# Modulation blocks as row dot products on DVE, another cost table for the planner, and an earlier normalization of the first tile in the last stage

## The chip, the cores and the metric

The kernel runs on one core of a Trainium2 chip. The metric is the device time of one execution in microseconds. The kernel before was timed in three runs.

## The reference

The input is a sequence of 256 tokens with 1024 features, `x`, a conditioning vector `c`, memory tokens and the weights, all float32. Two blocks of two layers each follow one another. In the first block each layer `i` is conditioned by `c`; this is the part that the change touches:

```
sc = jax.nn.silu(c)
for i in range(2):
    mod = sc @ w_ada[i] + b_ada[i]                  # 6 blocks of 1024
    sh_m, sc_m, g_m, sh_f, sc_f, g_f = split(mod, 6)
    h = rms_norm(x, norm_mix[i]) * (1 + sc_m) + sh_m
    y = moba_attention(h, ...) if i == 0 else short_conv(h, w_in, conv_w, w_out)
    x = x + g_m * y
    h = rms_norm(x, norm_ffn[i]) * (1 + sc_f) + sh_f
    x = x + g_f * swiglu(h, w_gate_up[i], w_down[i])
```

The second block has two layers with a gated linear recurrence and a stick-breaking attention, each with a memory attention beside it, a projection, a layer norm, and a mixture of 16 experts with a layer norm. The last layer norm gives the output.

## The kernel before

The 256 tokens are two tiles, T0 and T1, of 128 rows (`x0` and `x1` in the trace and the order). Both go through eight stages: attention, first FFN, short conv, second FFN, recurrence, first MoE, stick-breaking attention, second MoE. All weights come from DRAM as 556 units of 128x1024 floats (512 KB each) on SP's queue into a ring of buffers; `pump` issues the loads. A dense unit (`raw`) is split in two fp32r parts: ACT casts it to `hi`, DVE subtracts to get `lo` (line L487 is the helper `tt`). A product is then three fp32r matmuls, of `hi` with both parts of the left side and of `lo` with its first part. Left sides are made from a tile by `modnorm`: ACT squares the tile with an accumulated sum, DVE, POOL (a power) and DVE again scale it, PE transposes it in two times four 128x128 pieces, ACT applies scale and shift from `mcol`, and ACT's cast and a DVE subtraction split it.

Which instruction an engine gets next is decided before the run, by a planner in Python, `Sched`. Each part of the work is a generator that yields conditions; the planner keeps a clock `now` for PE and further clocks `tA`, `tD` for ACT and DVE, and `dma_t` for the loads, adds a cost for each instruction it emits (`mm` and `tr` for PE, `pump` for a load), and always continues the part that can go on first by these clocks. The costs are a table of numbers written into those functions. The order so found is fixed; on the chip each engine runs its own list in order, and semaphores make it wait for the others.

`ada_task` makes the modulation `mod`, in twelve blocks (i, j) of 1024 outputs. Five blocks, `ADA_PE`, go through PE as they are. For the other seven, (0,5) and all six of layer 1, each of the eight units of a block holds 128 of the 1024 input rows; DVE multiplies a unit by the matching column of `cs` = silu(c) and adds it to a sum `dst` of 128x1024. The sum over the 128 partitions is left to PE: for shifts and scales with eight 128x1 matmuls against a column `one`, four for each half block (the trace shows 64 for four blocks in eight sets), after which DVE adds the bias and writes `mcol`; for the gates ((0,5), (1,2), (1,5)) POOL first clears `dst` and loads the bias into a row of it, and each half is split (ACT, DVE) and multiplied twice with `ones`, so that the sum stands in all partitions.

The last stage ends with two layer norms: for T0 in `affine_pool` (normalization on ACT, then gain and bias of the left half on POOL and of the right half on DVE), for T1 in `affine_rows` (four operations on DVE); `moe` starts them.

Of the kernel before, what the change touches and what calls it, by code (L numbers as in the profile page):

```python
# [9 lines left out]
F32R = mybir.dt.float32r  # L10
# [14 lines left out]
GATES = (2, 5)  # L25
# [136 lines left out]
def host_arrays(inp):  # L162
# [3 lines left out]
    for i in range(2):  # L166
        for j in range(6):
            w = np.ascontiguousarray(g["w_ada"][i][:, j * D:(j + 1) * D])
            u[f"ada{i}_{j}"] = _split_units(w) if (i, j) in ADA_PE else w.reshape(8, 128, 1024)
# [27 lines left out]
    rows = np.stack([rowsrc[s] for k, (s, i) in zip(plan.kind, plan.src) if k == "row"])  # L197
# [104 lines left out]
class Body:  # L302
# [28 lines left out]
    def start(self, again):  # L331
# [21 lines left out]
        self.rawdense = 0  # L353
        self.hl_used = 0
# [96 lines left out]
    def mm(self, out, lhsT, rhs, start, stop, shared=False):  # L451
        self.nc.tensor.matmul(out, lhsT, rhs, start=start, stop=stop, skip_group_check=shared)  # L452
        n = 1
        for d in rhs.shape[1:]:
            n *= d
        m = out.shape[0]
        if lhsT.dtype == F32R:
            c = max(0.227 * n / 512, 0.108)
        else:
            c = max(0.86 * n / 512, 0.224 if m > 64 else 0.112) * (0.26 if m <= 32 and n == 512 else 0.52 if m <= 64 and n == 512 else 1.0)  # L460
        self.sch.now += c

    def tr(self, out, in_):
        self.nc.tensor.transpose(out, in_, self.ident)  # L464
        self.sch.now += 0.109
# [71 lines left out]
    def pump(self):  # L537
        while self.can_dma():
# [18 lines left out]
            self.dma_t = max(self.dma_t, self.sch.now) + 1.3  # L557
# [141 lines left out]
    def ada_task(self):  # L699
        for i in range(2):  # L700
            order = [(j, (b,)) for b in range(2) for j in (1, 0)] if i == 0 else [(1, (0, 1)), (0, (0, 1))]
            for j, halves in order + [(j, (0, 1)) for j in (2, 4, 3, 5)]:
                uid = self.ids[f"ada{i}_{j}"]
                gate = j in GATES
                onpe = (i, j) in ADA_PE
                dst = None
                if gate or not onpe:
                    yield [self.gate(uid[0]), self.rS(1)]
                    dst = self.tS()
                if gate:  # L710
                    self.nc.gpsimd.memset(dst, 0.0)
                    self.nc.gpsimd.dma_start(dst[0:1, :], self.bada_d[6 * i + j:6 * i + j + 1])
                    yield 4.0
# [9 lines left out]
                for b in halves:  # L723
                    d = dst[:, b * 512:(b + 1) * 512] if dst is not None else None
                    if onpe:
                        yield [self.gate(uid[4 * b + 3]), self.unit(uid[4 * b + 3]), self.bk(1)] + ([] if gate else [self.rH(1)])
                        bank = self.bank()
                        for q in range(4):
                            raw = self.take(uid[4 * b + q]).rearrange("p (k n) -> p k n", k=2)
                            for kk in range(2):  # L730
                                k = 2 * q + kk
                                gq = k % 4
                                self.mm(bank[32 * gq:32 * gq + 32], self.cs[:, k:k + 1].to_broadcast([128, 32]), raw[:, kk], k < 4, k >= 4)
                            self.done(uid[4 * b + q])
                        if gate:
                            self.tt(d, bank, d, ALU.add)
                        else:
                            d = self.tH()
                            self.scopy(d, bank)
                        self.free()  # L740
                    if gate:
                        yield [self.rH(3)]
                        hi, lo = self.tH(F32R), self.tH(F32R)
                        ones = self.ones
                        if onpe:
                            ones = self.tH(F32R)[:, :128]
                            self.vcopy(ones, self.sel4[:, 0:1].to_broadcast([128, 128]))
                        self.split(hi, lo, d)
                        yield [self.w(), self.bk(1)]
                        bank = self.bank()  # L750
                        self.mm(bank, ones, hi, True, False)
                        self.mm(bank, ones, lo, False, True)
                        self.fH(3 if onpe else 2)
                        self.scopy(d, bank)
                    else:
                        yield [self.w(), self.bk(1)]
                        bank = self.bank()
                        m = self.mcol[:, i, j, 4 * b:4 * b + 4]
                        c = V_BA + 48 * i + 8 * j + 4 * b
                        if onpe:  # L760
                            for q in range(4):
                                self.tr(bank[:, q * 128:(q + 1) * 128], d[:, q * 128:(q + 1) * 128])
                            self.fH()
                            self.red(m, bank.rearrange("p (q g e) -> p q g e", q=4, e=32)[:, :, :, 0], ALU.add)
                            self.tt(m, m, self.vecs[:, c:c + 4], ALU.add)
                        else:
                            for q in range(4):
# [3 lines left out]
                        if j in (1, 4):  # L771
                            c = V_NG + 16 * i + (8 if j == 4 else 0) + 4 * b
                            self.stt(m, m, 1.0, self.vecs[:, c:c + 4], ALU.add, ALU.mult)
                        self.sch.ev[f"mod{i}_{j}_{b}"] = self.chain + 0.12
                    self.free()
                if gate:
                    self.mod[i, j] = dst
                    self.set(f"mod{i}_{j}")
                elif dst is not None:
                    self.fS()  # L780
# [523 lines left out]
    def affine_pool(self, T, nm, src):  # L1304
# [978 lines left out]
```

## Time and profile before

| | us |
|---|---|
| three runs: median (lowest to highest) | 1204.48 (1203.82 to 1207.32) |
| the profiled execution, its own time | 1204.19 |
| its span in the trace | 1202.4 |
| PE busy | 1144.9 (95%) |
| DVE busy | 725.0 (60%) |
| ACT busy | 549.1 (46%) |
| POOL busy | 44.8 (4%) |
| mean granted PE clock, 1 is full speed | 0.988 |

The span is the time from the first to the last event in the trace. A busy time is the sum over an engine's instructions, with overlaps counted once. Weight loads of PE overlap its matmuls. In the timelines below, a row is a start, a duration, an engine, a line of the kernel, an operation and its operands, where `bk` is a PSUM bank, `tS` and `tH` are working tiles and `raw`, `hi`, `lo` are units; in brackets stands how long the engine was idle ahead of it and what it waited for. A matmul's duration reaches to the end of its result; since matmuls are pipelined, their pace is read from the starts.

### The profile page before, as it was taken

The page shows a single profiled execution, that of the slowest core. Times are in us where ns is not written, and L with a number is a line of the kernel's source. Part 1 is how long each engine was busy: PE and PEld are TensorE (multiplying, and loading weights), DVE is VectorE, ACT ScalarE, POOL GpSimd, SP SyncE. Part 2 cuts the span into 40 slices and gives each one's busy share as a digit, 9 for nine tenths or more (in the row PEclk, how much of TensorE's full clock was granted, in tenths as well). Part 3 has the DMA queues.
Part 4 walks back from the last instruction along what each step waited for, and adds up shares of the span by engine and source line. Part 5 has one row for each costly group of instructions (what it writes and reads, how often), then busy time and mean ns, then how long its engine had stood idle before and what let it go on. Part 6 is the DMA issues. An engine that isn't in the chain of part 4 may idle for free. (4 is left out here: it accounts for less than half of the span.)

```text
span 1202.4 us, 16685 instructions
## 1 busy us (share of the span) xinstructions
PE 1144.9 (95%) x6344; PEld 823.7 (69%) x6344; DVE 725.0 (60%) x1121; ACT 549.1 (46%) x913; POOL 44.8 (4%) x65
## 2 busy tenths in 40 slices
PE   7999989999998999999999999999999899999995
PEld 4777768888886787788887789886333577673331
DVE  4577667667577987665556567678221766564214
ACT  4655465434446455544434484553121456631211
POOL 0021000000000000000000000100000100000001
PEclk9999999999999999999999999999999899999998
DMA  9976768777664866466556233377999842587994
GB/s 375 409 306 228 256 222 302 262 268 269 244 239 155 340 247 215 158 211 217 205 194 209 86 125 105 123 277 266 378 409 408 311 142 72 188 333 306 408 408 159
DMA packets 83544, 301.72 MB, mean 251 GB/s; under 512 B 9408, under 2 KB 9824, under 8 KB 83456
## 3 DMA queue, kind: packets, MB, share of 16 engines
q1 hardware_dynamic: 82224, 298.37, 67.1%
q0 software_dynamic: 944, 1.82, 0.6%
q8 instruction: 52, 0.85, 0.3%
q10 hardware_dynamic: 288, 0.38, 0.1%
q14 instruction: 36, 0.29, 0.1%
HBM read 298.83 MB, written 2.10 MB: 250 GB/s over the span
## 5 line engine op out<-in xcount | busy, mean ns | idle before, releaser
L452 PE MATMUL bk<-hi,tS 128*128 128x512 f32 (+1 forms) x1760 | 586.9, 399 | 13.7 <-ACT hi L506 8.0
L452 PEld LDWEIGHTS bk<-hi,tS 128*128 128x128 f32 x1760 | 332.6, 190 | 87.2 <-ACT hi L506 8.7
L487 DVE TENSOR_TENSOR lo<-raw,hi 128x1024 fp32r<-128x1024 f32 x266 | 317.1, 1221 | 67.4 <-ACT hi L506 65.7
L452 PE MATMUL bk<-lo,tS 128*128 128x512 f32 (+1 forms) x880 | 345.0, 392 | 1.6 <-DVE lo L487 1.6
L506 ACT CAST hi<-raw 128x1024 fp32r<-128x1024 f32 x263 | 265.0, 1049 | 20.8 <-DMA raw<-in_units_dram 8.2
L452 PEld LDWEIGHTS bk<-lo,tS 128*128 128x128 f32 x880 | 167.4, 190 | 35.0 <-DVE lo L487 3.4
L480 ACT ACTIVATE tH<-bk 128x256 f32<-128x256 f32 (+1 forms) x100 | 44.8, 449 | 253.8 <-PE bk L452 253.6
L452 PE MATMUL bk<-hi,tH 128*128 128x512 f32 x384 | 133.1, 397 | 1.4 <-ACT tH L506 1.4
L487 DVE TENSOR_TENSOR tH<-tH,bk 128x256 f32<-128x256 f32 x60 | 25.1, 419 | 143.4 <-ACT tH L480 143.3
L452 PE MATMUL bk<-raw,tB 128*32 128x512 f32 x768 | 89.1, 594 | 0.4 <-DVE tB L494 0.4
L452 PEld LDWEIGHTS bk<-hi,tH 128*128 128x128 f32 x384 | 72.3, 189 | 17.1 <-ACT tH L506 2.1
L452 PE MATMUL bk<-raw,tH 128*32 128x512 f32 x640 | 80.1, 594 | 0.6 <-DMA raw<-in_units_dram 0.5
L452 PE MATMUL bk<-lo,tH 128*128 128x512 f32 x192 | 75.1, 391 | 0.0
L498 DVE SCALAR_TENSOR_TENSOR tS<-raw,cs,tS 128x1024 f32<-128x1024 f32 x52 | 66.6, 1280 | 0.3
L452 PEld LDWEIGHTS bk<-raw,tB 128*32 128x32 f32 x768 | 23.2, 110 | 52.4 <-issue 45.9
L498 DVE SCALAR_TENSOR_TENSOR tS<-bk,gsl,tS 128x512 fp32r<-128x512 f32 x32 | 23.3, 749 | 56.2 <-ACT tS L480 55.8
L464 PE MATMUL bk<-identr,tH 128*128 128x128 f32 x296 | 49.9, 277 | 6.8 <-DVE tH L487 3.0
L452 PEld LDWEIGHTS bk<-raw,tH 128*32 128x32 f32 x640 | 22.1, 109 | 49.0 <-issue 39.8
L464 PEld LDWEIGHTS bk<-identr,tH 128*128 128x128 f32 x296 | 36.1, 140 | 28.1 <-issue 8.2
L506 ACT CAST tH<-bk 128x256 fp32r<-128x256 f32 (+1 forms) x52 | 18.5, 356 | 67.5 <-PE bk L464 65.3
L480 ACT ACTIVATE tS<-bk,gsl 128x512 fp32r<-128x512 f32 x32 | 21.1, 686 | 60.7 <-PE bk L452 60.7
L506 ACT COPY tH<-bk 128x256 f32<-128x256 f32 (+1 forms) x56 | 25.6, 474 | 49.0 <-PE bk L452 38.6
(197 smaller groups left out, 990.8 us busy)
## 6 DMA issues: line engine op xcount, KB each, us to landing
raw<-in_units_dram SPq DMA_DIRECT2D x556, 512.0 KB, 5.7
row<-in_rows_dram SPq DMA_DIRECT2D x9, 512.0 KB, 7.6
x<-in_x_dram SPq DMA_DIRECT2D x2, 512.0 KB, 9.6
xsave<-x POOLq DMA_DIRECT2D x2, 512.0 KB, 5.0
out_dram<-x SPq DMA_DIRECT2D x3, 256.0 KB, 2.0
ulv<-in_ulv_dram POOLq DMA_DIRECT2D x1, 384.0 KB, 7.2
cst<-in_consts_dram SPq DMA_DIRECT2D x1, 274.0 KB, 11.2
out_dram<-x ACTq DMA_DIRECT2D x1, 256.0 KB, 2.0
```

What stands on the lines that cost most here:

```text
L452: self.nc.tensor.matmul(out, lhsT, rhs, start=start, stop=stop, skip_group_check=shared)
L464: self.nc.tensor.transpose(out, in_, self.ident)
L480: self.nc.scalar.activation(out, in_, func, scale=scale)
L487: self.nc.vector.tensor_tensor(out, a, b, op)
L498: self.nc.vector.scalar_tensor_tensor(out, a, s, b, op0, op1)
L506: self.nc.scalar.copy(out, a)
```

## The change

Three things change.

First, for the seven blocks the host stores the transposed block, so that a unit holds 128 outputs with all 1024 inputs. A row of `c` is loaded into all partitions (one more 512 KB transfer on SP's queue), ACT applies Silu to it (`crow`), and it is held through the whole task. For each unit DVE forms the 128 dot products in one operation with an accumulated output, straight into a column of `mcol`; `ada_column` adds the bias. A gate's eight columns are brought to all partitions by eight transposes of a broadcast column on PE and two copies on ACT. The sums over partitions by PE, the splits of the gates' halves and POOL's clearing and bias loads for these blocks go.

Second, the planner's costs change: an fp32r matmul of 512 columns from 0.227 to 0.216, a transpose from 0.109 to 0.07, a load from 1.3 to 1.46, and some details of fp32 matmuls.

Third, in the last stage T0's normalization on ACT stands ahead of the event `fin` that it used to wait for (that event says that T1's statistics are issued); what waits for `fin` now is the gain and bias on POOL and DVE. DVE's two operations on T0 are issued one ahead of T1's four and one behind.

```diff
-            u[f"ada{i}_{j}"] = _split_units(w) if (i, j) in ADA_PE else w.reshape(8, 128, 1024)
+            u[f"ada{i}_{j}"] = _split_units(w) if (i, j) in ADA_PE else np.ascontiguousarray(w.T).reshape(8, 128, 1024)
...
-    rows = np.stack([rowsrc[s] for k, (s, i) in zip(plan.kind, plan.src) if k == "row"])
+    rows = np.stack([rowsrc[s] for k, (s, i) in zip(plan.kind, plan.src) if k == "row"] + [g["c"][0]])
...
-            c = max(0.227 * n / 512, 0.108)
+            c = 0.216 * max(n, 512 if n < 256 else n) / 512
...
-        self.sch.now += 0.109
+        self.sch.now += 0.07
...
-                if not onpe:
-                    for k in range(8):
-                        yield [self.gate(uid[k]), self.unit(uid[k]), lambda: self.tD - 0.8]
-                        w = self.take(uid[k])
-                        if k or gate:
-                            self.stt(dst, w, self.cs[:, k:k + 1], dst, ALU.mult, ALU.add)
-                        else:
-                            self.ts(dst, w, self.cs[:, k:k + 1], None, ALU.mult, None)
-                        self.done(uid[k])
...
-                        self.split(hi, lo, d)
-                        yield [self.w(), self.bk(1)]
-                        bank = self.bank()
-                        self.mm(bank, ones, hi, True, False)
-                        self.mm(bank, ones, lo, False, True)
...
-                            for q in range(4):
-                                self.mm(bank[:, q:q + 1], d[:, q * 128:(q + 1) * 128], self.one, True, True)
-                                self.sch.now += 0.1
-                            self.tt(m, bank[:, :4], self.vecs[:, c:c + 4], ALU.add)
...
+                if (i, j) in ADA_PE:
+                    yield from self.ada_streamed(i, j, halves, uid)
+                else:
+                    if self.crow is None:
+                        yield [self.gate(uid[0]), self.rS(1)]
+                        self.crow = self.tS()
+                        r = self.rows_d[self.rows_d.shape[0] - 1]
+                        self.nc.sync.dma_start(self.crow, bass.AP(tensor=r.tensor, offset=r.offset, ap=[[0, 128], [1, 1024]]))
+                        self.dma_t = max(self.dma_t, self.sch.now) + 1.3
+                        t = self.dma_t + 2.0
+                        yield lambda: t
+                        self.act(self.crow, self.crow, AF.Silu)
+                        yield self.w()
+                    yield from self.ada_dots(i, j, uid)
+        self.fS()
+
+    def ada_column(self, i, j, b):
+
+        m = self.mcol[:, i, j, 4 * b:4 * b + 4]
+        c = V_BA + 48 * i + 8 * j + 4 * b
+        self.tt(m, m, self.vecs[:, c:c + 4], ALU.add)
+        if j in (1, 4):
+            c = V_NG + 16 * i + (8 if j == 4 else 0) + 4 * b
+            self.stt(m, m, 1.0, self.vecs[:, c:c + 4], ALU.add, ALU.mult)
+
+    def ada_dots(self, i, j, uid):
+
+        for b in range(2):
+            for q in range(4 * b, 4 * b + 4):
+                yield [self.gate(uid[q]), self.unit(uid[q]), lambda: self.tD - 0.8]
+                w = self.take(uid[q])
+                self.nc.vector.scalar_tensor_tensor(w, w, 1.0, self.crow, ALU.mult, ALU.mult,
+                                                    accum_out=self.mcol[:, i, j, q:q + 1])
+                self.onD(1024)
+                self.chain = self.tD = self.tD + 0.1
+                self.done(uid[q])
+            self.ada_column(i, j, b)
+            if j not in GATES:
+                self.sch.ev[f"mod{i}_{j}_{b}"] = self.chain + 0.12
+        if j in GATES:
+            yield [self.w(), self.rS(1)]
+            dst = self.tS()
+            for b in range(2):
+                yield self.bk(1)
+                bank = self.bank()
+                for q in range(4):
+                    k = 4 * b + q
+                    self.tr(bank[:, q * 128:(q + 1) * 128], self.mcol[:, i, j, k:k + 1].to_broadcast([128, 128]))
+                self.scopy(dst[:, b * 512:(b + 1) * 512], bank)
+                self.free()
+            self.mod[i, j] = dst
+            self.set(f"mod{i}_{j}")
...
@@ -1311,13 +1339,14 @@
             self.act(x[:, c], src[b], AF.Identity, bias=nb, scale=sv[:, 2:3])
+        yield f"fin{nm}"
...
         self.nc.scalar.dma_start(self.out_d[T][:, :512], x[:, :512])
-        yield f"sent{nm}"
         for op, r in ops:
             self.tt(x[:, 512:], x[:, 512:], r[:, 512:], op)
+            yield f"sent{nm}"
         self.send(T, slice(512, 1024))
...
         if T == 0 and self.last[T]:
-            yield f"fin{layer}"
             yield from self.affine_pool(T, f"f{layer}", acc)
         else:
-            self.sch.set(f"fin{layer}")
+            self.sch.set(f"finf{layer}")
```

The changed costs and the changed work move instructions on every engine. Three places follow, with numbers on tiles and units, since the rows would read alike without them.

PE between the first FFN and the conv layer. `bk_1725`, `bk_1726` are T0's sums of the FFN, `bk_1832`, `bk_1833` T1's, `bk_3187` and `bk_3188` products of T1's next slice of that FFN. The kernel before, its last matmuls ahead of T0's transposes (`tS_3257`) and what follows:

```order
L452 MATMUL bk_3187<-lo_3112,tS_1708 128x512
L452 MATMUL bk_3187<-hi_3111,tS_1709 128x512
L464 MATMUL bk_3265<-identr_84,tH_3252 128x128 x2
L464 MATMUL bk_3277<-identr_84,tS_3257 128x128 x4
L464 MATMUL bk_3288<-identr_84,tS_3257 128x128 x4
L452 MATMUL bk_1832<-hi_3122,tH_3268 128x512
L452 MATMUL bk_1832<-lo_3123,tH_3268 128x512
```

The change, with T0's transposes (`tS_3211`) and those of a gate's columns (`mcol`):

```order
L453 MATMUL bk_3188<-lo_3069,tS_1707 128x512
L453 MATMUL bk_3188<-hi_3068,tS_1708 128x512
L465 MATMUL bk_3242<-identr_84,tS_3211 128x128 x4
L465 MATMUL bk_3253<-identr_84,tS_3211 128x128 x4
L465 MATMUL bk_3268<-identr_84,mcol_91 128x128 x4
L465 MATMUL bk_3274<-identr_84,mcol_91 128x128 x4
L465 MATMUL bk_3280<-identr_84,tH_3239 128x128 x2
L453 MATMUL bk_3287<-hi_3108,tS_3209 128x512
```

Between T0's last matmul of the FFN and its transposes stood 12 matmuls of T1 before, and 30 stand there now; behind the transposes stood 12 of T1's down products (the first two are shown), and now ten small transposes stand there, ahead of the conv layer's products on T0's new left side (`tS_3209`).

PE between the conv layer and the second FFN. `bk_4151` is T1's second half of the output projection, on the left side `tS_3454`, `tS_3455`. The kernel before, with the end of 24 matmuls of T1 and T0's transposes (`tS_4172`):

```order
L452 MATMUL bk_4151<-hi_4064,tS_3454 128x512
L452 MATMUL bk_4151<-lo_4065,tS_3454 128x512
L452 MATMUL bk_4151<-hi_4064,tS_3455 128x512
L464 MATMUL bk_4199<-identr_84,tS_4172 128x128 x4
L464 MATMUL bk_4210<-identr_84,tS_4172 128x128 x4
L452 MATMUL bk_4231<-hi_4095,tS_4170 128x512
```

The change, where `bk_4007` is T0's second half of the output projection, and `bk_4020` T1's first:

```order
L453 MATMUL bk_4007<-hi_4003,tS_3265 128x512
L453 MATMUL bk_4007<-lo_4004,tS_3265 128x512
L453 MATMUL bk_4007<-hi_4003,tS_3266 128x512
L465 MATMUL bk_4097<-identr_84,tS_4086 128x128 x4
L465 MATMUL bk_4108<-identr_84,tS_4086 128x128 x4
L453 MATMUL bk_4020<-hi_3861,tS_3458 128x512
```

T0's own projection now ends directly ahead of its transposes; T1's products, which lay between, come behind them.

DVE at the same place. `x0_82` is T0, and `tS_4172` its scaled form that the transposes read. The kernel before:

```order
L487 TENSOR_TENSOR tH_4144<-bk_4080,tS_2902 128x512
L487 TENSOR_TENSOR x0_82<-x0_82,tH_4144 128x512
L487 TENSOR_TENSOR lo_4148<-raw_4045,hi_4147 128x1024
L494 TENSOR_SCALAR tm_4176<-tm_4173 128x1
L492 TENSOR_SCALAR tS_4172<-x0_82,tm_4175 128x1024
L487 TENSOR_TENSOR tH_4196<-bk_4151,tS_2902 128x512
```

The change, where `tB` is a tile of T1's conv and `tS_4086` the scaled form of T0:

```order
L488 TENSOR_TENSOR tH_4071<-bk_4007,tS_3267 128x512
L488 TENSOR_TENSOR x0_82<-x0_82,tH_4071 128x512
L488 TENSOR_TENSOR lo_4075<-raw_3960,hi_4074 128x1024
L499 SCALAR_TENSOR_TENSOR tB_3457<-tB_3457,vecs_78 128x127
L499 SCALAR_TENSOR_TENSOR tB_3457<-tB_3264,vecs_78,tB_3457 128x1
L499 SCALAR_TENSOR_TENSOR tB_3457<-tB_3457,vecs_78 128x126
L499 SCALAR_TENSOR_TENSOR tB_3457<-tB_3264,vecs_78,tB_3457 128x2
L495 TENSOR_SCALAR tm_4090<-tm_4087 128x1
L493 TENSOR_SCALAR tS_4086<-x0_82,tm_4089 128x1024
L488 TENSOR_TENSOR tB_3457<-tB_3457 128x512
L488 TENSOR_TENSOR tS_3459<-tB_3457,tS_3458 128x512
```

A split alone stood between T0's residual and its scaling before; four conv operations of T1 stand there too now, and the end of T1's conv, which its products (`tS_3459`) need, stands behind it.

## Rows read from the trace of the kernel before

**Rows 1.** The page: busy us of each engine, share of the span, instructions.

```profile
PE 1144.9 (95%) x6344; PEld 823.7 (69%) x6344; DVE 725.0 (60%) x1121; ACT 549.1 (46%) x913; POOL 44.8 (4%) x65
```

**Rows 2.** What PE waited for, whole span: releaser, us in total, times, longest.

```profile
PE bk L452 <- ACT hi L506: 8.0, 2, 7.2
...
PE bk L452 <- DMA raw<-in_units_dram: 0.5, 2, 0.2
```

**Rows 3.** Stretch 400:480: busy us (count) of PE, PEld, DVE, ACT, POOL; clock, DMA, GB/s.

```profile
400.00:480.00 80.00, 75.89 (x359) 62.07 (x358) 66.34 (x110) 42.08 (x67) 1.10 (x2) 0.98 0.71 258
```

**Rows 4.** PE's timeline around one set of `one` matmuls: start, us, row.

```profile
263.31 0.62 PE L452 MATMUL bk<-hi,tS 128*128 128x512 f32 x2
...
263.99 0.39 PE L452 MATMUL bk<-hi,tS 128*128 128x512 f32 x1
264.22 0.94 PE L452 MATMUL bk<-one,tS 128*128 128x1 f32 x8
...
265.35 0.40 PE L452 MATMUL bk<-lo,tS 128*128 128x512 f32 x1
```

**Rows 5.** PE's timeline at one gate half.

```profile
222.76 0.62 PE L452 MATMUL bk<-tH,ones 128*128 128x512 f32 x2
223.22 0.40 PE L452 MATMUL bk<-hi,tS 128*128 128x512 f32 x1
```

**Rows 6.** PE's timeline at two small transposes.

```profile
269.90 0.39 PE L452 MATMUL bk<-hi,tS 128*128 128x512 f32 x1
270.13 0.38 PE L464 MATMUL bk<-identr,tH 128*128 128x128 f32 x2
...
270.58 0.39 PE L452 MATMUL bk<-lo,tS 128*128 128x512 f32 x1
```

**Rows 7.** Groups by line and form: count, busy us, mean ns, idle before.

```profile
L487 DVE TENSOR_TENSOR lo<-raw,hi 128x1024 fp32r<-128x1024 f32 x266 | 317.1, 1221 | 67.4 <-ACT hi L506 65.7 <-DMA raw<-in_units_dram 0.3
...
L498 DVE SCALAR_TENSOR_TENSOR tS<-raw,cs,tS 128x1024 f32<-128x1024 f32 x52 | 66.6, 1280 | 0.3
...
L492 DVE TENSOR_SCALAR tS<-raw,cs 128x1024 f32<-128x1024 f32 x4 | 3.0, 747 | 0.0
...
L478 ACT ACTIVATION_READ_ACCUMULATOR tS<-x 128x1 f32 x8 | 1.5, 189 | 0.0
```

**Rows 8.** PE's timeline between the first FFN and the conv layer.

```profile
363.71 0.44 PE L464 MATMUL bk<-identr,tH 128*128 128x128 f32 x2 [0.93 <-DVE tH L487]
366.01 1.06 PE L464 MATMUL bk<-identr,tS 128*128 128x128 f32 x8 [1.86 <-DVE tS L492]
```

**Rows 9.** Timelines of PE, DVE, ACT between conv and second FFN.

```profile
472.90 1.03 PE L464 MATMUL bk<-identr,tS 128*128 128x128 f32 x8
475.74 0.50 PE L452 MATMUL bk<-hi,tS 128*128 128x512 f32 x1 [1.81 <-ACT tS L506]
...
484.69 0.50 PE L452 MATMUL bk<-hi,tS 128*128 128x512 f32 x1 [0.44 <-ACT tS L506]
...
467.65 0.69 DVE L487 TENSOR_TENSOR tH<-bk,tS 128x512 f32<-128x512 f32 x1
...
471.17 0.76 DVE L492 TENSOR_SCALAR tS<-x,tm 128x1024 f32<-128x1024 f32 x1 [0.66 <-POOL tm L521]
...
469.17 1.06 ACT L478 ACTIVATE tS<-x 128x1024 f32<-128x1024 f32 x1 [4.59 <-DVE x L487]
```

**Rows 10.** Two windows at the seams, columns as in rows 3.

```profile
476.00:481.00 5.00, 5.00 (x15) 3.65 (x15) 2.61 (x5) 4.97 (x10) 0.55 (x1) 0.66 0.49 175
360.00:367.00 7.00, 4.21 (x24) 3.19 (x23) 5.63 (x10) 1.74 (x4) 0.56 (x1) 1.00 1.03 411
```

**Rows 11.** PE's timeline at the first MoE's start.

```profile
942.86 0.66 PE L464 MATMUL bk<-identr,x 128*128 128x128 f32 x4 [1.08 <-DVE x L498]
```

**Rows 12.** The end: PE's last matmul and DVE's last operations.

```profile
1188.70 0.50 PE L452 MATMUL bk<-tS 128*128 128x512 f32 x1 [0.28 <-DVE tS L498]
...
1193.59 2.47 DVE L487 TENSOR_TENSOR x<-x,row 128x512 f32<-128x512 f32 x2
```

More of the change, by code (lines that the diff above doesn't have):

```diff
@@ L353, in start @@
         self.rawdense = 0
+        self.crow = None
         self.hl_used = 0
@@ L457, in mm @@
         if lhsT.dtype == F32R:
-            c = max(0.227 * n / 512, 0.108)
+            c = 0.216 * max(n, 512 if n < 256 else n) / 512
         else:
-            c = max(0.86 * n / 512, 0.224 if m > 64 else 0.112) * (0.26 if m <= 32 and n == 512 else 0.52 if m <= 64 and n == 512 else 1.0)
+            c = max(0.858 * n / 512, 0.11) * (0.26 if m <= 32 and n == 512 else 0.53 if m <= 64 else 1.0)
         self.sch.now += c
@@ L556, in pump @@
             self.tiles[i] = t
-            self.dma_t = max(self.dma_t, self.sch.now) + 1.3
+            self.dma_t = max(self.dma_t, self.sch.now) + 1.46
             self.arr[i] = self.dma_t + 2.0
@@ L723, in ada_task @@
[L723 to L726, printed above, removed]
-                        bank = self.bank()
-                        for q in range(4):
[L729 to L747, printed above, removed]
-                        self.split(hi, lo, d)
-                        yield [self.w(), self.bk(1)]
-                        bank = self.bank()
-                        self.mm(bank, ones, hi, True, False)
-                        self.mm(bank, ones, lo, False, True)
[L753 to L767, printed above, removed]
-                                self.mm(bank[:, q:q + 1], d[:, q * 128:(q + 1) * 128], self.one, True, True)
-                                self.sch.now += 0.1
-                            self.tt(m, bank[:, :4], self.vecs[:, c:c + 4], ALU.add)
[L771 to L780, printed above, removed]
+                if (i, j) in ADA_PE:
[12 more added lines that the diff above has]
+                    yield from self.ada_dots(i, j, uid)
@@ new lines, in ada_streamed @@
+    def ada_streamed(self, i, j, halves, uid):
+        gate = j in GATES
+        dst = None
+        if gate:
+            yield [self.gate(uid[0]), self.rS(1)]
+            dst = self.tS()
+            self.nc.gpsimd.memset(dst, 0.0)
+            self.nc.gpsimd.dma_start(dst[0:1, :], self.bada_d[6 * i + j:6 * i + j + 1])
+            yield 4.0
+        for b in halves:
+            d = dst[:, b * 512:(b + 1) * 512] if gate else None
+            yield [self.gate(uid[4 * b + 3]), self.unit(uid[4 * b + 3]), self.bk(1)] + ([] if gate else [self.rH(1)])
+            bank = self.bank()
+            for q in range(4):
+                raw = self.take(uid[4 * b + q]).rearrange("p (k n) -> p k n", k=2)
+                for kk in range(2):
+                    k = 2 * q + kk
+                    gq = k % 4
+                    self.mm(bank[32 * gq:32 * gq + 32], self.cs[:, k:k + 1].to_broadcast([128, 32]), raw[:, kk], k < 4, k >= 4)
+                self.done(uid[4 * b + q])
+            if gate:
+                self.tt(d, bank, d, ALU.add)
+            else:
+                d = self.tH()
+                self.scopy(d, bank)
+            self.free()
+            if gate:
+                yield [self.rH(3)]
+                hi, lo = self.tH(F32R), self.tH(F32R)
+                ones = self.tH(F32R)[:, :128]
+                self.vcopy(ones, self.sel4[:, 0:1].to_broadcast([128, 128]))
+                self.split(hi, lo, d)
+                yield [self.w(), self.bk(1)]
+                bank = self.bank()
+                self.mm(bank, ones, hi, True, False)
+                self.mm(bank, ones, lo, False, True)
+                self.fH(3)
+                self.scopy(d, bank)
+            else:
+                yield [self.w(), self.bk(1)]
+                bank = self.bank()
+                for q in range(4):
+                    self.tr(bank[:, q * 128:(q + 1) * 128], d[:, q * 128:(q + 1) * 128])
+                self.fH()
+                self.red(self.mcol[:, i, j, 4 * b:4 * b + 4], bank.rearrange("p (q g e) -> p q g e", q=4, e=32)[:, :, :, 0], ALU.add)
+                self.ada_column(i, j, b)
+                self.sch.ev[f"mod{i}_{j}_{b}"] = self.chain + 0.12
+            self.free()
+        if gate:
+            self.mod[i, j] = dst
+            self.set(f"mod{i}_{j}")
```

10 lines of the change are left out of this document (removed).

## The prediction

> **What bounds the kernel now.** I read four views in this order. The page first [rows 1]: PE is busy 1144.9 of 1202.4 us, DVE 725.0. So PE sets the time, and what counts is work taken from it, or time in which it stands still. The profiled execution took 1204.19 us, 1.79 more than its span and 0.29 under the median of the three runs, 1204.48. Second, what PE waits for [rows 2]: no releaser gives more than 8.0 us in all, 7.2 of that in one wait, and DMA 0.5. The waits are many and short, at the seams between stages; there a new instruction order wins or loses a few us at a time. Third, busy time by stretches of 80 us from 160 to 640, where the edited modulation work lies: the fullest for DVE is 400 to 480, 66.3 of 80 [rows 3], so DVE has slack. Fourth, PE's timeline at the edited places.
>
> **Term 1, modulation work on PE: -7.1 us.** An fp32r matmul starts every 0.227 us in a full stream (263.31 to 263.99 for three [rows 4]). A non-gate block ended in two sets of eight 128x1 matmuls. Around one set [rows 4] the stream goes on at 265.35 with the second matmul after the one at 263.99: 1.36 us for two steps of 0.227, so the set cost 0.9. Eight sets: 7.2. A gate half had two matmuls against `ones`, 222.76 to 223.22 [rows 5], 0.46; six halves: 2.7. Added are 24 transposes. Two transposes at 270.13 let the stream take 0.68 from 269.90 to 270.58 for two steps [rows 6], 0.23 too much, 0.115 each: 24 make 2.8. Net -7.2 - 2.7 + 2.8 = -7.1. Bounds: at 0.07 or 0.13 a transpose -8.2 and -6.8. PE is full there, so the saving reaches the end unless a later wait takes it; weights land early enough (0.5 us on DMA [rows 2]).
>
> **Term 2, the dots on DVE: 0.** Removed are 52 operations of 1280 ns and 4 of 747 [rows 7], 69.5 us; added are 56 of the former's shape, at least 71.7. What an accumulated output adds no DVE row of this kernel shows; the nearest is ACT's readout of an accumulator, 189 ns [rows 7]. So 1.28 to 1.47 us each, 2 to 13 in all. Six splits of 128x512 go, at some 0.69 each like the operation of that size in [rows 9]; 14 additions on a few columns come, and I take them to cost what those splits did. DVE gains up to 13 us over 450 in which it has at least 13.7 free of every 80 [rows 3], and PE hides that; without the cover a dot ahead of a norm would hold PE by up to 1.5 us. One more row of 512 KB on SP's queue comes ahead of loads that are early (DMA 0.5 us [rows 2]), and one Silu on ACT, over 1 us like the square of [rows 9], once: 0. POOL's three memsets and bias loads go; nothing waited for them: 0.
> The trace shows 1280 ns for this operation with two f32 SBUF sources and 747 for the form with one [rows 7], and I put the dots at the former. [...]
>
> **Term 3, order at the seam of the first FFN and the conv layer: -1.7 us.** Before, 12 matmuls of T1 follow T0's last one of this FFN, then PE waits 0.93 and 1.86 [rows 8] for T0's norm: residual, square, DVE, POOL, DVE. By the rows of the next seam [rows 9] it takes four residual operations of 0.69, 2.0 from the square's start to the scale's, and 0.76: 5.5 us. In the new order 30 matmuls (6.8 us) stand ahead of the transposes, so the 2.8 go. But behind the transposes only ten small ones (1.1 us) cover the affine and the split, which took from 472.90 to 475.74 at the next seam [rows 9], 2.8 us, of which the transposes themselves hide 0.8: about 1.1 of wait is new (0 to 2). Net -1.7, bounds -2.8 and 0.
>
> **Term 4, order at the seam of conv and the second FFN: +6.2 us.** Here the new order looks worse. Before, 24 matmuls of T1 follow T0's output projection and hide T0's norm: PE enters the transposes at 472.90 without a wait. [...] After, T0's last 18 projection matmuls run straight into T0's transposes. PE must stand through two residual operations (0.69 each), 2.0 from the square's start to the scale's, and the scale's 0.76 [rows 9]: 4.2 us. DVE holds a split (1.22 [rows 7]) and four conv operations between residual and scale, about 1 us more than the square covers: 5.2 (4.3 to 6.0). T1's matmuls then wait about 0.5 for the rest of its conv, which DVE does after the scale (0.4 to 0.7). T1's norm has six matmuls ahead of its transposes; the nearest case, twelve, gave 0.93 + 1.86 [rows 8], so 2.8 (2.0 to 3.5). The clock falls once, 1.7, or twice, 3.4; I take once. Sum 5.2 + 0.5 + 2.8 + 1.7 = 10.2, less 4.0: +6.2, bounds +4.4 and +9.6.
>
> **Term 5, smaller moves: +2.2 us.** In the conv stage a set of four transposes follows its own tile's matmuls, where six matmuls of the other tile lay between: +0.8. At the first MoE 28 matmuls of T1 lie beside T0's norm and not 34; PE waited there already, 1.08 at one place [rows 11], so six fewer cost up to 6 x 0.227 = 1.4. Other swaps (the recurrence, the MoE's down products) I can give no sign. For all of these -2 to +4. From the first MoE to the end the order is nearly the same.
>
> **Term 6, the end: -0.6 us.** PE's last matmul starts at 1188.70, and DVE ends at 1193.59 + 2.47 = 1196.06 [rows 12]. Those last two operations on T0 took 2.47, while a residual's of the same size takes 0.69 [rows 9]; the first ran beside POOL. With one of them ahead of T1's four, before POOL begins, and the other after POOL's end, up to 1.1 us go. Against it: the early normalization puts a small DVE operation, which waits for POOL's power (0.66 [rows 9]), ahead of the product that PE's last matmul waits for; about 0.2 later, and 0.3 is left in doubt beside it. Net -0.6, bounds -1.1 and +0.3.
>
> **Sum.** -7.1 + 0 - 1.7 + 6.2 + 2.2 - 0.6 = -1.0, and 1204.19 - 1.0 = 1203.2 us. A measurement of this kernel can tell about 0.3%, 3.6 us, from no change; so I forecast none.
>
> **The rivals.**
> A, the forecast: PE's saving is eaten by the uncovered norm at the second seam. 1203.2; own range 1200 to 1208.
> B, the saving passes. The DVE and ACT parts of the norms lie further ahead of PE than I count (term 4 only +2, term 5 at 0): -7.1 - 1.7 + 2 - 0.6 = -7.4, 1196.8. For it: PE is 95% busy and its work shrinks for certain. Against: nothing at all stands between projection and transposes.
> C, the other side: the new standstill at the second seam lowers the clock twice. Terms 4 and 5 at their upper bounds, term 3 at 0: -7.1 + 9.6 + 4 - 0.6 = +5.9, 1210.1. It decides once that seam holds over 12 us of standing and slow clock. For it: 1.81 us of standing sufficed for a fall at this seam [rows 9, 10]. Against: 2.8 at the first seam, in two parts, left it at 1.00 [rows 10].
> [...]
> E, that the change doesn't do what it says, the dots still needing PE as before: the order shows no 128x1 matmul of them left, so it has no chance of its own.
>
> **How the numbers follow.** A 0.42, B 0.32, C 0.20, D 0.06. Of A 0.35 lie within 0.3%, 0.04 are faster, 0.03 slower. With B faster 0.36; with C and D slower 0.29; same 0.35. A's own range holds about half of what can be; 1195 to 1212 takes in B and C but for their outer ends, and leaves out D.
>
> **What would show it.** Term 1: no 128x1 matmuls of this kind, and PE's busy time down by some 7 us. [...] Term 3: no 0.93 and 1.86 ahead of the conv layer's transposes, one wait near 1 behind them. Term 4: over 4 us of idle PE ahead of T0's transposes for the second FFN, some 3 ahead of T1's, the granted clock below 1 behind them; under 2 in all and I am wrong towards B. Term 6: T0's last add takes 0.7 us on DVE.

## The result and the profile after

The changed kernel is slower: 1214.68 us (median of 4 runs, 1214.06 to 1215.69) against 1205.66 us for the kernel before in the same comparison; ratio 1.0077, 95% interval 1.0062 to 1.0091, some 9 us. The profiled execution of the change spans 1212.3 us, 9.9 more than that of before. The time lies above the range that I gave.

The page's row of busy times, which answers to [rows 1]:

```profile
PE 1143.6 (94%) x6292; PEld 824.0 (68%) x6292; DVE 720.8 (59%) x1179; ACT 544.9 (45%) x906; POOL 41.0 (3%) x59
```

PE is busy 1.3 us less than before, and I had said 7. Its work did shrink; the rest is that a busy time counts slow matmuls in full (eight transposes took 1.97 us at 457.45, with a granted clock of 0.51, and 1.03 at 355.84, with 1.00), and the mean granted clock fell from 0.988 to 0.980. In the tenth experiment below, which has the same 6292 matmuls at a mean clock of 0.985, PE is busy 1137.1 us, 7.8 less than before.

The groups by line and form, of what the modulation does now (count, busy us, mean ns, idle before), against [rows 7]:

```profile
L736 DVE SCALAR_TENSOR_TENSOR raw<-raw,tS 128x1024 f32<-128x1024 f32 x56 | 67.8, 1218 | 0.0
...
L736 DVE DVE_READ_ACCUMULATOR raw<-raw,tS 128x1 f32 x56 | 4.6, 82 | 0.0
...
L465 PE MATMUL bk<-identr,mcol 128*128 128x128 f32 x24 | 3.1, 272 | 0.0
```

A dot takes 1218 ns, and the readout of its accumulator, an instruction of its own, 82 ns: 1.30 us, near the lower end of what I allowed. 56 of them make 72.4 us, against 69.5 us for the operations they replace. DVE's busy time did not rise; it is 720.8 us in all.

What PE waited for, whole span (us in total, times, longest), against [rows 2]:

```profile
PE bk L465 <- DVE tS L493: 8.4, 3, 5.8
PE bk L453 <- DVE lo L488: 6.7, 4, 4.9
...
PE bk L453 <- ACT tS L481: 2.6, 1, 2.6
```

Three single waits stand out: one of 5.8 us on a scaled tile, one of 4.9 on a split, and one of 2.6 on ACT's silu. None of these had a counterpart of that length before: the longest on the same three releasers were 1.9, 0.5 and 0.2. They lie in three places.

**Between the conv layer and the second FFN.** PE's timeline, against [rows 9]:

```profile
451.24 0.39 PE L453 MATMUL bk<-hi,tS 128*128 128x512 f32 x1
457.45 1.97 PE L465 MATMUL bk<-identr,tS 128*128 128x128 f32 x8 [5.82 <-DVE tS L493]
...
475.42 0.44 PE L465 MATMUL bk<-identr,tH 128*128 128x128 f32 x2 [1.62 <-DVE tH L488]
476.98 1.09 PE L465 MATMUL bk<-identr,tS 128*128 128x128 f32 x8 [1.12 <-DVE tS L493]
```

and DVE's at the same place:

```profile
452.57 0.69 DVE L488 TENSOR_TENSOR tH<-bk,tS 128x512 f32<-128x512 f32 x1
...
455.04 0.87 DVE L499 SCALAR_TENSOR_TENSOR tB<-tB,vecs 128x127 f32<-128x127 f32 x4
...
456.64 0.75 DVE L493 TENSOR_SCALAR tS<-x,tm 128x1024 f32<-128x1024 f32 x1 [0.66 <-POOL tm L522]
```

and the window behind the wait (columns as in [rows 3]):

```profile
456.00:461.00 5.00, 3.55 (x13) 3.17 (x14) 2.26 (x4) 2.94 (x7) 0.55 (x1) 0.51 0.02 3
```

T0's projection ends with the matmul at 451.24. The residual, the square, four conv operations and the scale follow, and PE goes on at 457.45, after 5.82 us. The clock granted from 456 to 461 is 0.51. At T1's norm PE then stands 1.62 and 1.12 us, and the clock falls a second time:

```profile
470.00:480.00 10.00, 7.26 (x33) 5.56 (x32) 4.15 (x8) 4.08 (x10) 0.55 (x1) 0.90 0.49 157
480.00:486.00 6.00, 6.00 (x25) 4.91 (x24) 4.37 (x5) 4.72 (x8) 0.00 (x0) 0.88 0.25 87
```

**In the recurrence.** PE's timeline:

```profile
767.62 2.50 PE L453 MATMUL bk<-tB,tS 128*128 128x128 f32 x12 [3.15 <-DVE tB L488]
...
785.83 0.58 PE L453 MATMUL bk<-lo,tS 128*128 128x256 f32 x1 [4.93 <-DVE lo L488]
```

DVE's timeline ahead of the second of these waits:

```profile
778.88 1.10 DVE L511 TENSOR_REDUCE tm<-tH 128x4 f32<-128x512 f32 x2 [3.64 <-ACT tH L481]
...
781.63 1.02 DVE L488 TENSOR_TENSOR tS<-bk,tm 128x512 f32<-128x512 f32 x2 [1.45 <-POOL tm L522]
...
784.55 4.62 DVE L488 TENSOR_TENSOR lo<-raw,hi 128x1024 fp32r<-128x1024 f32 x4
```

DVE's list has T1's norm (the reduce, a wait of 1.45 on POOL, two products and two more operations) ahead of four splits, and PE needs the first of the splits. The 5 us are not the whole of it. The row at 767.62 is T1's last step of the recurrence. From there to the first MoE, the window of the change:

```profile
767.62:816.37 48.75, 41.93 (x240) 35.47 (x241) 29.48 (x50) 24.07 (x48) 2.26 (x3) 0.89 0.45 162
```

and of the kernel before, from the same step at 761.41 to the same point:

```profile
761.41:809.85 48.44, 47.87 (x287) 40.52 (x288) 33.73 (x53) 28.23 (x53) 2.26 (x3) 1.00 0.64 228
```

The stretches last equally long, 48.8 and 48.4 us. But in the change PE does 240 matmuls and transposes in it, where it did 287; 48 matmuls of 512 columns (10.9 us at 0.227) had been done ahead of the step instead, and behind it PE stands or runs slowly, at a clock of 0.89. The stretch ahead of the step, which opens with eight transposes of `x`, is longer by that work, here the kernel before and then the change:

```profile
664.22:761.41 97.19, 91.80 (x530) 79.47 (x528) 64.62 (x103) 56.39 (x99) 2.84 (x3) 0.98 0.32 103
658.78:767.62 108.84, 103.05 (x577) 88.42 (x575) 68.84 (x106) 60.19 (x104) 2.83 (x3) 0.98 0.38 131
```

Both stretches together took 145.6 us before and take 157.6 in the change.

**At the end.** ACT's timeline of the change:

```profile
1195.49 1.45 ACT L485 ACTIVATE x<-bk,tm,stat 128x512 f32<-128x512 f32 x2 [3.46 <-DVE tm L495]
1196.83 0.69 ACT L481 ACTIVATE tS<-bk,gsl 128x512 fp32r<-128x512 f32 x1
```

PE's:

```profile
1194.21 0.73 PE L453 MATMUL bk<-tS 128*128 128x512 f32 x2
1197.57 0.50 PE L453 MATMUL bk<-tS 128*128 128x512 f32 x1 [2.62 <-ACT tS L481]
```

DVE's:

```profile
1200.23 0.68 DVE L488 TENSOR_TENSOR x<-x,row 128x512 f32<-128x512 f32 x1
...
1204.70 0.68 DVE L488 TENSOR_TENSOR x<-x,row 128x512 f32<-128x512 f32 x1
1205.30 0.14 DVE L503 CAST go<-flag 1x1 int32<-1x1 f32 x1
```

The same places in the kernel before, PE:

```profile
1186.96 0.73 PE L452 MATMUL bk<-tS 128*128 128x512 f32 x2
1187.91 0.51 PE L452 MATMUL bk<-tS 128*128 128x512 f32 x1 [0.22 <-ACT tS L480]
```

and DVE's last operation:

```profile
1195.97 0.13 DVE L502 CAST go<-flag 1x1 int32<-1x1 f32 x1
```

Before, 0.95 us lay between the pair of matmuls at 1186.96 and the next. In the change it is 3.36, since T0's normalization on ACT stands ahead of the last silu and waits itself for POOL and DVE. DVE's operations on T0 are indeed short now, 0.68 each and not 2.47 together [rows 12]. From the pair to DVE's last operation it was 9.01 us and is 11.09.

### The profile page after: what moved, and what is told of

It is laid out like the page before. It is cut to its first block, busy times and chain, and to the rows that moved or that the text cites. A ratio compares the mean times of both kernels' runs of the same rounds, so it can differ in the third digit from the quotient of the medians.

```text
span 1212.3 us, 16559 instructions
## 1 busy us (share of the span) xinstructions
PE 1143.6 (94%) x6292; PEld 824.0 (68%) x6292; DVE 720.8 (59%) x1179; ACT 544.9 (45%) x906; POOL 41.0 (3%) x59
## 3 DMA queue, kind: packets, MB, share of 16 engines
q0 software_dynamic: 848, 1.81, 0.5%
## 5 line engine op out<-in xcount | busy, mean ns | idle before, releaser
L736 DVE SCALAR_TENSOR_TENSOR raw<-raw,tS 128x1024 f32<-128x1024 f32 x56 | 67.8, 1218 | 0.0
```

What stands on the lines that cost most here:

```text
L736: self.nc.vector.scalar_tensor_tensor(w, w, 1.0, self.crow, ALU.mult, ALU.mult, accum_out=self.mcol[:, i, j, q:q + 1])
```

## The experiments

All ratios are to the kernel before, with their 95% intervals; a ratio's per cent is 12 us.

**1. The dots alone.** The old costs and the old end, with the dots of the change.

```diff
-            c = 0.216 * max(n, 512 if n < 256 else n) / 512
+            c = max(0.227 * n / 512, 0.108)
...
-        self.sch.now += 0.07
+        self.sch.now += 0.109
...
-            self.dma_t = max(self.dma_t, self.sch.now) + 1.46
+            self.dma_t = max(self.dma_t, self.sch.now) + 1.3
```

(and the old `affine_pool` and `moe`)

> The dots alone, with the planner's old costs and the old end. The order of PE is that of the kernel before but for the modulation work itself and the seam of conv and second FFN, where T0's projection runs straight into T0's transposes as in the change. Theory (the dots move that seam, not the cost table): PE work falls by 7.1 us, the seam costs the 9.1 us that the trace of the change shows there, so +2 against before (0 to +4), with one PE wait of 5 to 6 us on DVE's scaled tile near 450 us and no wait of 4.9 us on a lo near 780 us. Rival (all that got slower came with the cost table or the end): -7, no long wait near 450.

Measured: 1.0006 (0.9995 to 1.0016), +0.7 us. PE's order matched that of before except for the modulation, this seam and a few matmuls near 320 us, and the wait was there, 5.78 us long:

```profile
463.04 1.97 PE L465 MATMUL bk<-identr,tS 128*128 128x128 f32 x8 [5.78 <-DVE tS L493]
```

No wait of that length on a split appears in the recurrence. So the uncovered seam comes with the dots, not with the cost table.

**2. The dots, with T1's conv first in the planner.**

```diff
-            self.sch.spawn(conv(b), 0.2 + 0.1 * T)
+            self.sch.spawn(conv(b), 0.2 + 0.1 * T if T == 0 else -0.5)
```

> As e1_dots, but T1's conv has the planner's highest priority, so that T1's projection can lie between T0's projection and T0's transposes again (24 matmuls, as before). Theory: the wait of 5 to 6 us and the slow clock behind it go, -7 against before (-5 to -9), 9 us under e1_dots. Rival (the seam is not worth what the trace's gaps say, since a wait there is paid back later): within 3 us of e1_dots.

Measured: 0.9954 (0.9941 to 0.9966), -5.5 us; median 1199.17 against 1205.29 without the edit, 6.1 us. PE goes straight into T0's transposes again:

```profile
467.11 1.03 PE L465 MATMUL bk<-identr,tS 128*128 128x128 f32 x8
469.95 0.50 PE L453 MATMUL bk<-hi,tS 128*128 128x512 f32 x1 [1.81 <-ACT tS L507]
```

Both of its parts hold: the dots, with the seam covered, take some 6 us off the program, and the seam without cover takes 6 back. Read by position the seam is worth 5.6: the four small transposes ahead of it start at 447.10 in the first experiment and at 447.46 here, two of those behind it at 500.44 and 495.24. The gaps in the change's trace had promised 9.1; a third of that does not show. There the clock fell twice at this seam, but in the first experiment it is back at 1.00 behind the second wait (482.8 to 487.5), which is some 1.7 of the difference.

**3. The end alone.** The kernel before with the two edits of `affine_pool` and `moe` that the change makes.

> The kernel before with the new end alone; the order up to the last silu is that of before. Theory (ACT's early normalization stands ahead of the last silu, waits for POOL and DVE, and holds up PE's last matmuls): +2.2 us against before (PE's end +2.6, the DVE part behind it -0.4). Rival (my prediction's term 6): -0.6 us.

Measured: 1.0021 (1.0012 to 1.0030), +2.5 us. PE waits as in the change:

```profile
1186.66 0.73 PE L452 MATMUL bk<-tS 128*128 128x512 f32 x2
1190.00 0.50 PE L452 MATMUL bk<-tS 128*128 128x512 f32 x1 [2.61 <-ACT tS L480]
```

**4. The end, with the normalization behind the last silu.**

```diff
         if T == 0 and self.last[T]:
+            yield f"moe{layer}_1_0"
             yield from self.affine_pool(T, f"f{layer}", acc)
```

> As e3_new_end, but the early normalization is issued only behind the last silu; DVE's two operations on T0 stay one ahead of T1's four and one behind. Theory: PE's end as before, and DVE's operation that took 1.74 us beside POOL takes 0.7, so -1 us against before (-0.3 to -1.5); 3 us under e3_new_end. Rival (what costs at the end is the DVE order, not ACT's): as e3_new_end.

Measured: 0.9995 (0.9984 to 1.0007), no difference that can be told, and 3.1 us under the new end. PE and DVE:

```profile
1187.68 0.73 PE L452 MATMUL bk<-tS 128*128 128x512 f32 x2
1188.64 0.50 PE L452 MATMUL bk<-tS 128*128 128x512 f32 x1 [0.22 <-ACT tS L480]
```

```profile
1191.06 0.69 DVE L487 TENSOR_TENSOR x<-x,row 128x512 f32<-128x512 f32 x1
...
1195.54 0.68 DVE L487 TENSOR_TENSOR x<-x,row 128x512 f32<-128x512 f32 x1
1196.14 0.13 DVE L502 CAST go<-flag 1x1 int32<-1x1 f32 x1
```

From the pair to DVE's last operation it is 8.46 us, 0.55 less than before. That piece of my term 6, DVE's two operations away from POOL's, is real, but half of the 1.1 that I gave it: T0's product takes 0.69 where it took 1.74, and an operation of T1 (`x<-x,stat,row`), which now runs beside POOL's, takes 1.43 where it took 0.75. ACT's place in front of the silu is what I had not counted.

**5. The new costs of matmuls and transposes, only from the recurrence on**, on top of the dots with T1's conv first.

```diff
-            c = max(0.227 * n / 512, 0.108)
+            c = 0.216 * max(n, 512 if n < 256 else n) / 512 if self.late else max(0.227 * n / 512, 0.108)
...
     def layer2(self, T):
+        self.late = True
```

> e2_dots_conv_first with the planner's new costs of matmuls and transposes switched on where the recurrence's stage begins; up to there the order is that of e2_dots_conv_first, and in the recurrence the order of DVE is that of the change (both tiles' norm before four splits). Theory (the new costs open the wait on a split in the recurrence): a PE wait of about 5 us on a lo, 11.6 us over e2_dots_conv_first by the gaps in the change's trace, so +5.5 against before (+3 to +7). Rival (that wait comes from the dots or from late data): as e2_dots_conv_first, -6.

Measured: 1.0042 (1.0027 to 1.0056), +5.1 us, 10.6 over the kernel it was made from. Up to the recurrence its order is that kernel's. The waits are those of the change, with matmuls behind T1's last step again 48 fewer:

```profile
766.78 2.58 PE L454 MATMUL bk<-tB,tS 128*128 128x128 f32 x12 [3.15 <-DVE tB L491]
...
784.97 0.58 PE L454 MATMUL bk<-lo,tS 128*128 128x256 f32 x1 [4.92 <-DVE lo L491]
```

**6. The same, with the splits earlier.** Seven splits may be issued up to 6 us earlier by the planner's clocks.

```diff
-                return max(self.arr[i], min(self.tA, self.tD) - 1.15)
+                early = 6.0 if 226 <= j <= 232 and not self.again else 1.15
+                return max(self.arr[i], min(self.tA, self.tD) - early)
```

> As e5_costs_late, but the planner may issue seven splits of the recurrence's last units and the first of its projection up to 6 us earlier, so that they stand ahead of T1's norm on DVE. Theory (the split's place in DVE's list is what PE waited for): the 5 us wait goes, and 7 us or more of the 11.6 come back: -2 against before (-5 to +1). Rival (PE would wait there anyway, for the norm itself): within 2 us of e5_costs_late.

Measured: 1.0034 (1.0023 to 1.0044), +4.1 us, within 1.2 us of the one before it. My theory of this experiment fell. The wait on the split is gone, and PE stands as long elsewhere, for the softmax of a memory attention on DVE:

```profile
769.67 1.60 PE L454 MATMUL bk<-tB,tS 128*128 128x128 f32 x12 [0.56 <-DVE tB L491]
...
796.27 1.09 PE L468 MATMUL bk<-identr,tH 128*128 128x128 f32 x4 [5.10 <-DVE tH L491]
```

PE had done still more ahead of T1's last step here: 54 matmuls of 512 columns were left behind it, against 72 in the change and 120 before. The stretch from T1's last step to the first MoE lasts 44.0 us here, 4.9 less than in the fifth experiment, but that step comes 2.9 later. So the split was where PE stood, not why; what is missing is work beside T1's last chain. The run does not show this by itself, since the edit moved the work as well as the wait; the tenth does.

**7. The new costs up to the recurrence only**, on top of the dots with T1's conv first: the condition of the fifth experiment turned round (`if not self.late`).

> e2_dots_conv_first with the new costs of matmuls and transposes up to the recurrence and the old ones from there. The order in the recurrence and behind it is that of e2_dots_conv_first. Theory (the change's trace has 2.9 us less lost at the attention's end and some 2.8 less at the first seam; both from the costs): 3 to 5 us under e2_dots_conv_first, -9 to -11 against before. Rival (those gains were chance or belong to the dots): within 1.5 us of e2_dots_conv_first; the seam of conv and second FFN has 18 and 12 matmuls of cover here and not 24 and 18, which may cost up to 2.

Measured: 0.9967 (0.9952 to 0.9981), -4.0 us, which is 1.6 over the kernel without the new costs, though its runs spread widely (1197.53 to 1204.01). The theory fell: no gain from the new costs shows here.

**8. The new cost table alone**: the kernel before with the new costs of matmuls, transposes and loads.

> The kernel before with the whole new cost table, old modulation and old end. The seam of conv and second FFN keeps its cover (36 matmuls). Two splits stand right behind T1's scaling in the recurrence, not four behind both norms. Theory: gains of 3 to 5 us before the recurrence, a wait in it of some 2 to 5 with slow clock, net -2 to +4 against before; no wait of 5 us near 450. Rival (the table alone makes what the change lost): +9 or more.

Measured: 1.0035 (1.0021 to 1.0049), +4.2 us. Just above what I expected; half of what the change lost. Behind T1's last step stand 96 matmuls of 512 columns.

**9. The change with the old end**: its `affine_pool` and `moe` are those of the kernel before.

> The change with the old end; PE's order up to the end is the change's. Theory (the new end costs 2.5 us by e3_new_end): +6.5 against before (+5 to +8). Rival (the end costs nothing here, since the first part's delay hides it): +9.

Measured: 1.0050 (1.0036 to 1.0064), +6.0 us. The new end costs the change some 3 us.

**10. The change with the old costs from the recurrence on.** The edit is the fifth experiment's turned round: the old costs of matmuls and transposes stand where `self.late` holds. The new cost of a load stays throughout.

> The change, with the old costs of matmuls and transposes from the recurrence on; up to there its order is the change's, and from the recurrence's last step of T1 to the first MoE PE has 33.0 us of fp32r matmuls again (before the change 33.0, with it 22.1, counted from the order). Theory (the matmuls that PE does ahead of that step are missing behind it as cover): 10 to 12 us under the change, so -2 against before (-4 to 0). Rival (e6_costs_late_split_early showed that mending one wait there gains nothing, so PE stands elsewhere): +7 or more.

Measured: 0.9994 (0.9985 to 1.0002), -0.7 us, 10 us under the change. From T1's last step to the first MoE PE has 287 matmuls and transposes again, at full clock, and the stretch ahead of the step has its old length:

```profile
659.27:756.60 97.33, 92.05 (x530) 79.50 (x528) 63.86 (x101) 56.27 (x99) 2.83 (x3) 0.98 0.32 103
756.60:804.95 48.35, 47.79 (x287) 40.49 (x288) 33.69 (x53) 28.21 (x53) 2.27 (x3) 1.00 0.63 229
```

Together they take 145.7 us, as before. From there to the end of the span it is 396.4 us, and 395.9 in the change, so the 10 us lie in the recurrence. A load's cost has no part in this: the fifth experiment has the old one, the tenth the new one. Which of the other costs (fp32r matmuls, fp32 matmuls, transposes) does it was not tried.

**11. The dots with T1's conv first and the mended end**: the second and the fourth experiment's edits together.

> The dots with the old costs, T1's conv first, and the mended end of e4_end_mended. Theory (the two gains add up, at different places): -6.5 against before (-5 to -8). Rival (the end is then bound otherwise): as e2_dots_conv_first or slower.

Measured: 0.9969 (0.9959 to 0.9979), -3.7 us, 2.1 in the median above the kernel without the mended end (1201.32 and 1199.17). I had expected the opposite. The end itself is as in the fourth experiment: in both 8.46 us from the pair to DVE's last operation. The 3.4 us that its PE ends later in the trace have gathered before that, where both kernels have the same instructions: 1.4 by the first MoE, 2.6 by T0's transposes behind it (940.10 and 937.49), and the rest later; over 935 to 955 the granted clock was 0.83 here and 1.00 in the second experiment's trace. The two ran on different chips, and their intervals overlap; which is the better one stays open. Both beat the kernel before and the change.

**12. The change with T1's conv first**: the second experiment's edit on the change.

> The change with T1's conv first. The seam of conv and second FFN has 18 and 12 matmuls of cover instead of 0 and 6, and behind T1's last recurrence step stand 27.6 us of fp32r matmuls instead of 22.1. Theory (cover at both places is what the change lacks): 6 us less at the seam and up to 5 less in the recurrence, so +3 to -2 against before. Rival (the cover at the seam is paid back before the recurrence): +7 or more.

Measured: 1.0022 (1.0011 to 1.0032), +2.3 us, 6.7 under the change. 96 matmuls of 512 columns stand behind T1's last step. The edit moves both places here, so the run does not part them.

## Why the prediction was wrong

**Term 1, PE's modulation work (-7.1): right.** With the seam covered, the dots gave -5.5 us (-7.1 to -4.1 by the interval), and PE's busy time is 7.8 us lower in the tenth experiment; the 24 transposes are there, and no 128x1 matmul.

**Term 2, the dots cost nothing on DVE: right.** 1.30 us each with the readout: 1218 ns with an accumulator, and 82 for its readout, against 1280 before without one. D's chance of 0.06 was put on dots of twice 1.28 us; no run shows such a dot.

**Term 3, the first seam (-1.7): right in sign and place.** PE's timeline of the change:

```profile
355.84 1.03 PE L465 MATMUL bk<-identr,tS 128*128 128x128 f32 x8
...
358.68 0.50 PE L453 MATMUL bk<-hi,tS 128*128 128x512 f32 x1 [0.72 <-ACT tS L507]
```

The 0.93 and 1.86 ahead of the transposes [rows 8] are gone and 0.72 stands behind them: -2.1 by the waits. The dots alone do not bring it: in the first experiment PE still stands 0.93 and 1.91 us there, and in the tenth, with the new costs up to the recurrence, 0.71. What that is worth in the time was not tried by itself.

**Term 4, the second seam (+6.2): right in place, and in size partly by luck.** PE stands 5.8 us ahead of T0's transposes where I had 5.2, and 2.7 at T1 where I had 2.8. The 0.5 for the rest of T1's conv did not come: T1's matmuls start at 459.07, right behind T0's transposes. The 4.0 that the sum takes off is what the seam lost before: the waits of 1.81 and 0.44 [rows 9], and (1 - 0.66) x 5 = 1.7 by the clock of 0.66 over 476 to 481 [rows 10], which is also my price for one fall. The clock, which I let fall once, fell twice in the change's profiled execution; with 1.7 for each fall my own count gives 12.0 less 4.0, that is 8.0, and with one fall, as in the first experiment, 6.3. By the first two experiments the seam costs 6.1. I put it down to no part of the change; it comes with the dots.

**Term 5, "other swaps (the recurrence, the MoE's down products) I can give no sign", -2 to +4: wrong, and this step failed most.** The recurrence alone cost 10 to 11 us (the fifth and tenth experiments; 12.0 by its two stretches in the trace). I had compared the order only for waits that the trace of before showed. The order did show what mattered: 120 matmuls of 512 columns behind T1's last step before, 72 in the change. The new costs make the planner put 48 of them ahead of it, and behind it PE has too little to do beside T1's norm, memory attention and transposes. Why lower costs of PE lead the planner to that was not looked into further than the order. Of the two places that I did price in this term, the first MoE's does not show. The row that I read as its start, 942.86 [rows 11], stands behind that MoE, whose first router product is at 810.05; at the real start PE waits once for `x`, 0.65 us, in both kernels.

**Term 6, the end (-0.6): wrong in sign.** "A small DVE operation, which waits for POOL's power, ahead of the product that PE's last matmul waits for; about 0.2 later": I looked at DVE's list and not at ACT's. The two normalizations (1.45 us) and their own wait stand in front of the last silu. Measured +2.5 alone and about +3 in the change.

**The sum.** From the runs: dots with the open seam +0.7, costs from the recurrence on +10.6, end +2.5: +13.8. Against +9.3 by the ratio, the new costs ahead of the recurrence must give back about 4.5, and the tenth experiment says so: it has the dots, the new costs up to the recurrence (and that of a load), and the new end and is at -0.7, where the dots and the end alone make +3.2, so -3.9. Yet with T1's conv first the same costs took 1.6 (seventh experiment). An order found by a planner does not split into terms that add.

The forecast's own mechanism (A), the saving eaten by the uncovered norm at the second seam, is what the dots alone showed, +0.7; the table and the end came on top. Of the rivals, C was nearest: slower, by a new standstill and a slow clock behind it (0.51 over 456 to 461). But it had the wrong seam, and its price came from terms 4 and 5 at their upper bounds. Its sign, over 12 us of standing and slow clock at the second seam, was just about met in the profiled execution, with 12.0; yet that seam is worth 6.1 in the time. The larger loss lay in the recurrence, of which C says nothing.

## What to carry to other kernels

Where a planner fixes the order, count in the order how much work of the busiest engine stands behind each step on which the last tile's chain depends, before and after: a stretch bound by that chain can keep its length when the work is moved ahead of it (48.4 and 48.8 us here), and the moved work is then added to the time ahead (11.7 us). Mending the one wait at which the engine then stands gains little if the work beside it is missing (1.2 us here). When an operation is put earlier on an engine, read every operation behind it on that engine, not only on the engine that it was moved for.

## What was not expected of the hardware

An accumulating operation on DVE cost about the same as the plain one: 1218 ns and 82 for the readout, against 1280 ns for the same shape with a column and a tile as further operands.

The same waits did not always lower the clock. At the seam of attention and first FFN PE waits 1.39 and 1.41 us in the kernel before, and 1.39 and 1.45 in the change. Behind it the window 176 to 184 has, in the kernel before, a granted clock of 0.79, and in the change of 1.00:

```profile
176.00:184.00 8.00, 7.23 (x29) 6.22 (x30) 4.45 (x6) 6.04 (x12) 0.00 (x0) 0.79 0.20 66
176.00:184.00 8.00, 8.00 (x40) 6.74 (x39) 4.84 (x8) 6.06 (x12) 0.00 (x0) 1.00 0.46 153
```

That is 1.7 us of PE's time, but it is not a gain of the change. The change with the old end (9) has the change's waits there, and the kernel before with the mended end (4) has those of before; in their traces it is the other way round, 0.62 and 1.00:

```profile
176.00:184.00 8.00, 7.74 (x27) 6.51 (x27) 4.39 (x8) 6.05 (x12) 0.00 (x0) 0.62 0.21 66
176.00:184.00 8.00, 7.45 (x37) 6.36 (x38) 4.89 (x7) 6.06 (x12) 0.00 (x0) 1.00 0.35 129
```

So at this place the clock differed between executions with the same waits, and 1.7 to 3.0 us (0.21 and 0.38 of these 8) between two single traces need not come from the kernels.

A product and a sum on DVE between two SBUF tiles took 2.47 us together at the end of the kernel before, the first of them beside POOL's (1.74 and 0.69), and 0.68 each in the change, away from it. In the change it is one of T1's operations that runs beside POOL's, and it takes 1.44 us where it took 0.75.
